# Forgetting attention by head pairs on halves of TensorE, a packed low-rank projection, and another order of the last corrections, in a one-core layer kernel

## The chip, the cores and the metric

The kernel runs on one core of a Trainium2 chip. A core has five engines that run side by side: TensorE (PE; its weight loads are listed apart, as PEld), VectorE (DVE), ScalarE (ACT), GpSimd (POOL) and SyncE (SP). Each works through its own queue in order and waits for the others by semaphores. The metric is the device time of one execution in microseconds (us). Line numbers (L152) are those of the kernel before, unless the text says that they are of the changed kernel.

## What is computed

One layer of a streaming encoder for 512 frames of width 1024, in float32. After a norm, one wide projection feeds three branches (gated linear attention "GLA", forgetting attention "Fox", attention into 256 memory tokens); their outputs are gated and merged, projected and added to the input; a squared-ReLU MLP and a last norm follow. The part that the change touches most is the forgetting attention, 8 heads of 64 channels:

```python
def forgetting_attention(q, k, v, log_f):
    F = jnp.cumsum(log_f, axis=1)                  # per head
    ...
        s = jnp.einsum('bhqd,bhkd->bhqk', qi, kh) * scale
        s = s + Fi[..., None] - F[:, :, None, :]
        mask = k_pos[None, :] <= q_pos[:, None]
        p = jax.nn.softmax(jnp.where(mask, s, -jnp.inf), axis=-1)
        return jnp.einsum('bhqk,bhkd->bhqd', p, vh)
    ...
u = rmsnorm(h, g_mix[l]); proj = u @ w_in[l]       # 2*256+2*512+16+3*512+8+512+3*1024 columns
log_a = log_sigmoid(ga @ w_alpha_up[l] + b_alpha[l]) / GLA_TAU
log_f = log_sigmoid(ff + b_forget[l])
...
h = h + jnp.square(jax.nn.relu(u2 @ w_ff1[l])) @ w_ff2[l]
return rmsnorm(h, g_final)
```

## The kernel before

**Number format.** Large products are made of float32r matmuls. Each operand is split into a rounded part "hi" (a copy on ACT) and the rest "lo" (a subtraction on DVE); `split` (L202) and `split_w` (L139) do it. `mm3` (L150 to L153) then sums hi·hi, hi·lo and lo·hi into one PSUM tile: three matmuls for each 128 rows of contraction. Small products are plain float32.

**Stages, in the order of PE.** A front end (norms, keys and values for the memory), the low-rank and forget columns "G" (L388), the projections for Fox, then Fox itself woven with projections for GLA, memory attention woven with the merge of the Fox branch, GLA woven with the merge of the memory branch, the output projection, and the MLP in four quarters, each a Strassen-like scheme of seven products in the order 1, 2, 5, 6, 3, 7, 4 (L881).

**What sets the order.** PE runs in the order in which the code is written. The other engines' queues are ordered by the build's own scheduler. `weave` (L188) runs a list of attention steps and after each of them fills in its share of 128 units of projection work, a unit being three matmuls.

**G.** `run(gT(("G",), ...))` makes 8 times 3 matmuls from one weight chunk (16 low-rank columns, 8 forget columns, the rest zero) into `gaT`; a row of ones is set there (L383) so that the next small product adds the biases. Its first operand, the normed input `uhi`, `ulo`, is still being made at that time, a k at a time, by DVE (L367 and L204), ACT and POOL. Every weight chunk that goes through `split_w` also counts for `next_sum` (L120), which every second time starts a DMA from POOL that sums weights for the MLP in DRAM (tiles `T`).

**Fox.** `decay_logs` and `decay_sums` make F; `decay_rows` (L422) transposes it and writes -F by four small DMAs from ACT's queue to DRAM (`dF`); each head reads its row back to all partitions (`nFb`, L465). `fox_pair` (L438) projects q and k for two heads and lays them out so that one head uses all 128 rows: in Q the hi part lies on one half of the rows and the lo part on the other, and K's hi (then K's lo) lies on both halves. `fox_scores(h)` (L461) makes for each of four query blocks one matmul with K's hi, one bf16 matmul that adds the causal mask on the last 128 columns (L476), and one matmul with K's lo (L477); DVE adds `nFb` and finds the extreme (L479), ACT takes the exponential (L481), DVE divides by the row sum (L484). `fox_turn(h)` (L487) transposes the blocks on PE and splits them to `PTh`, `PTl`. `fox_values(h)` (L501) multiplies by `V`, whose hi and lo parts fill 64 columns each: eight matmuls a head; ACT and DVE add the two halves (L512, L516). In the woven list, head h's scores, head h-1's transposes and head h-2's values follow each other.

**Last quarter of the MLP.** `evac` (L1038) adds the seven products into the residual tiles `hN`, here `h` (two of them, t = 0 and 1, for each half of the rows; C(i, j, t) is a quarter). Some are added by DMAs from POOL that accumulate in place (`send`, L1035). `finish(t, c, n)` (L1015) takes one 512-column half of a row tile, squares it with a row sum on ACT, multiplies it by the gain, and with n = 1 also norms the tile and writes it out. All `finish` calls stand behind product 7 or 4, the last two.

## Time and profile before

| | |
|---|---|
| median of three timed runs | 855.12 us (853.72 to 855.91) |
| the profiled execution | 855.22 us, of it the span of the trace 853.5 us |
| instructions in the trace | 11749 |
| front end, until G's first matmul | 0 to 40.9 us |
| G and the projections for Fox | 40.9 to 95 us |
| Fox, first scores to last values | 95 to 213 us |
| memory attention and Fox's merge | 213 to 330 us |
| GLA and its merges, output projection, MLP | 330 to 838.2 us |
| after the last matmul | 838.2 to 853.5 us |

In the rows of the profile, a matmul's own duration is longer than the time to the next matmul's start, since matmuls are pipelined; what a stream of them costs is read from starts. A plain float32 matmul shows as two records, a float32r matmul as one. "Idle before" with a releaser says what an engine waited for.

### The profile page before, as it was taken

Reading aid. Unit: us, or ns where it says so; the run is one execution under the profiler, and the core shown is the slowest. Engines: PE = TensorE matmul, PEld = TensorE weight load, DVE = VectorE, ACT = ScalarE, POOL = GpSimd, SP = SyncE. Lnnn points to the kernel's source line nnn. Section 1 sums busy time; section 2 is a strip of 40 time slices with the busy share of each in tenths; the row PEclk is TensorE's granted clock in tenths of the full one; section 3 lists DMA queues with packets and bytes.
Section 4 is the critical chain, followed back from the end, with each engine's and each line's share of the span. In section 5 each row is a group of like instructions: output and inputs, shape, how many; then the busy total and the mean of one; then the engine's idle time right before and its main releaser. Section 6 shows DMA issues by size and latency. Waiting matters only on the chain.

```text
span 853.5 us, 11749 instructions
## 1 busy us (share of the span) xinstructions
PE 827.1 (97%) x4505; PEld 702.7 (82%) x4505; DVE 536.0 (63%) x820; ACT 439.8 (52%) x703; POOL 111.2 (13%) x124
## 2 busy tenths in 40 slices
PE   7999999999999999999999999999999999999992
PEld 5878788888888888878888889887997899799872
DVE  5784656746443545665443548475788678778964
ACT  7765656755233343323323436465676467457744
POOL 5200000000000001222121100111001000100243
PEclk9999999999999999999999999999999999999997
DMA  8444846544636556546322504768758956885694
GB/s 315 154 149 153 205 148 185 142 155 125 195 75 204 192 132 176 130 131 244 102 99 75 196 25 145 210 135 214 234 168 156 277 188 172 184 257 178 136 180 129
DMA packets 37513, 142.37 MB, mean 167 GB/s; under 512 B 4592, under 2 KB 5392, under 8 KB 35728
## 3 DMA queue, kind: packets, MB, share of 16 engines
q1 hardware_dynamic: 27216, 93.36, 31.5%
q0 software_dynamic: 8448, 45.09, 25.7%
q10 hardware_dynamic: 1792, 3.16, 1.2%
q8 instruction: 35, 0.57, 0.3%
q14 instruction: 22, 0.18, 0.1%
HBM read 136.34 MB, written 27.28 MB: 192 GB/s over the span
## 4 chain that ended last, share of the span: by engine, by line
PE 70%; issue 12%; DMA 8%; DVE 4%; ACT 3%; POOL 1%; SPq 0%; POOLq 0%; ACTq 0%; DVEq 0%
PE mm L152 20%; PE mm L151 19%; PE mm L153 19%; DMA b<-in_wst_dram 7%; PE a L152 2%; PE a L151 2%; PE a L153 2%; DVE lo L204 1%; ACT hi L203 1%; DMA h<-s 1%; POOL h L1036 1%; PE a L477 1%; DMA memr<-in_memT_dram 1%; PE a L508 1%; PE a L507 1%
## 5 line engine op out<-in xcount | busy, mean ns | idle before, releaser
L143 DVE TENSOR_TENSOR wlo<-raw,whi 128x1024 fp32r<-128x1024 f32 x80 | 101.4, 1271 | 107.6 <-ACT whi L142 106.6
L142 ACT CAST whi<-raw 128x1024 fp32r<-128x1024 f32 x80 | 84.1, 1052 | 136.4 <-PE mm L152 99.1
L151 PE MATMUL mm<-uhi,whi 128*128 128x512 f32 x360 | 142.6, 396 | 0.0
L152 PE MATMUL mm<-ulo,whi 128*128 128x512 f32 x360 | 140.7, 391 | 1.3 <-DVE ulo L204 1.3
L153 PE MATMUL mm<-uhi,wlo 128*128 128x512 f32 x360 | 140.5, 390 | 0.0
L203 ACT CAST hi<-raw 128x1024 fp32r<-128x1024 f32 x58 | 60.5, 1049 | 44.5 <-PE mm L152 31.6
L204 DVE TENSOR_TENSOR lo<-raw,hi 128x1024 fp32r<-128x1024 f32 x58 | 70.6, 1222 | 17.6 <-ACT hi L203 17.6
L152 PEld LDWEIGHTS mm<-ulo,whi 128*128 128x128 f32 x360 | 67.7, 188 | 15.8 <-DVE ulo L204 2.8
L153 PEld LDWEIGHTS mm<-uhi,wlo 128*128 128x128 f32 x360 | 67.6, 188 | 14.6 <-DVE wlo L143 0.4
L151 PEld LDWEIGHTS mm<-uhi,whi 128*128 128x128 f32 x360 | 67.7, 188 | 13.8 <-issue 0.5
L204 DVE TENSOR_TENSOR lo<-b,hi 128x1024 fp32r<-128x1024 f32 x40 | 48.9, 1223 | 37.2 <-ACT hi L203 37.2
L203 ACT CAST hi<-b 128x1024 fp32r<-128x1024 f32 x40 | 41.9, 1049 | 55.5 <-PE mm L153 22.6
L152 PE MATMUL mm<-lo,ch 128*128 128x512 f32 x160 | 63.0, 394 | 2.7 <-DVE lo L204 2.7
L151 PE MATMUL mm<-hi,ch 128*128 128x512 f32 x160 | 62.4, 390 | 0.0
L1036 POOL DMA_DIRECT2D b<-in_wst_dram x32 | 27.7, 866 | 266.4 <-DVE lo L204 210.4
L153 PE MATMUL mm<-hi,cl 128*128 128x512 f32 x160 | 62.3, 389 | 0.0
L153 PE MATMUL mm<-u2h,lo 128*128 128x256 f32 x192 | 54.3, 283 | 0.0
L152 PE MATMUL mm<-u2l,hi 128*128 128x256 f32 x192 | 54.3, 283 | 0.0
L151 PE MATMUL mm<-u2h,hi 128*128 128x256 f32 x192 | 54.3, 283 | 0.0
L151 PE MATMUL mm<-u2sh,hi 128*128 128x256 f32 x144 | 40.8, 283 | 0.0
L152 PE MATMUL mm<-u2sl,hi 128*128 128x256 f32 x144 | 40.8, 283 | 0.0
L153 PE MATMUL mm<-u2sh,lo 128*128 128x256 f32 x144 | 40.8, 283 | 0.0
(340 smaller groups left out, 1913.1 us busy)
## 6 DMA issues: line engine op xcount, KB each, us to landing
raw<-in_wst_dram SPq DMA_DIRECT2D x122, 512.0 KB, 3.7
b<-in_wst_dram POOLq DMA_DIRECT2D x32, 512.0 KB, 5.5
T<-in_wst_dram POOLq DMA_DIRECT2D x12, 1024.0 KB, 8.5
raw<-T SPq DMA_DIRECT2D x24, 512.0 KB, 3.5
b<-in_wst_dram SPq DMA_DIRECT2D x16, 512.0 KB, 4.9
xr<-in_xT_dram SPq DMA_DIRECT2D x4, 512.0 KB, 8.1
nFb<-dF ACTq DMA_DIRECT2D x8, 256.0 KB, 3.9
h<-in_xN_dram SPq DMA_DIRECT2D x4, 512.0 KB, 7.0
```

The costliest lines, as they stand in the source:

```text
L142: cast = nc.scalar.copy(hi, raw)
L143: nc.vector.tensor_tensor(lo, raw, f(hi), op=ALU.subtract)
L151: nc.tensor.matmul(ps, lh, rh, start=start, stop=False)
L152: nc.tensor.matmul(ps, lh, rl, start=False, stop=False)
L153: nc.tensor.matmul(ps, ll, rh, start=False, stop=stop)
L203: nc.scalar.copy(hi, src)
L204: return nc.vector.tensor_tensor(lo, src, f(hi), op=ALU.subtract).ins
L477: nc.tensor.matmul(ps[:, :w], q, K[e][:, 1, :w], start=False, stop=True)
L507: nc.tensor.matmul(po[:, q0:], vv, PTh[:, c0:c0 + w], start=n == 0, stop=False)
L508: nc.tensor.matmul(po[:, q0:], vv, PTl[:, c0:c0 + w], start=False, stop=n == 3)
L1036: nc.gpsimd.dma_start(to, x, accum_op=ALU.add)
```

## The change

**Fox.** Two heads, which are the two row halves of one projection tile, are now done together. `fox_pair` leaves q and k where the projection puts them (head 0 on rows 0 to 63, head 1 on rows 64 to 127), as tiles hi and lo: two operations for each tile. `fox_scores(j, i)` makes for query block i three float32r matmuls for each head, with 64 rows of contraction, in turn for the two heads and into two PSUM tiles. The mask matmul is gone: -F is written to DRAM in eight slots of 128 (seven writes; three blocks twice), read back as 7 x 128 columns for each head (`fox_rows`), and POOL adds the mask to the copies for the diagonal blocks. `fox_turn(e)` copies the transposed blocks out in float32 without a split. `fox_values(j)` makes plain float32 matmuls with 64 output columns, in turn for the two heads, which land on the two halves of the partitions of one PSUM tile. The woven list has 20 steps in place of 24: transposes of head 0, of head 1, scores for blocks 0 and 1, scores for blocks 2 and 3, values of the pair before.

**G.** The chunk's columns are stored twice; columns 64 to 127 are replaced by their lo part, so that 8 times 2 matmuls do the work, and the biases come in by a column of ones as the bias of the copy out of PSUM. It no longer goes through `split_w`, so it isn't counted for `next_sum`.

**Last quarter.** After product 6 DVE adds G to C(0, 1) itself and `finish(t, 0, 0)` follows at once; after product 3 DVE adds it from PSUM and `finish(t, 1, 1)` follows. Four accumulating DMAs of POOL go, two copies on ACT with them, and all gains are multiplied by DVE.

```diff
-        run(gT(("G",), uhi, ulo, ga_evac))
+        def low_rank():
+            raw = load_w(("G",))
+            both = wp.tile([P, 1024], F32R, tag="hi", name=nm("whi"))
+            raw3, w3 = (t.rearrange("p (k c) -> p k c", k=KT) for t in (raw, both))
+            nc.scalar.copy(both, raw)
+            low = slice(64, P)
+            nc.vector.tensor_tensor(w3[:, :, low], raw3[:, :, low], f(w3[:, :, low]), op=ALU.subtract)
+            ps = mmt()
+            for k in range(KT):
+                nc.tensor.matmul(ps, w3[:, k, :], uhi[:, k, :], start=k == 0, stop=False)
+                nc.tensor.matmul(ps, w3[:, k, :], ulo[:, k, :], start=False, stop=k == KT - 1)
+            nc.scalar.activation(gaT, ps, AF.Identity, bias=ones_row)
...
-            for t in range(NT):
-                nc.scalar.dma_start(dF[:, t * P:(t + 1) * P], nF[8 * t:8 * t + 8, :])
+            for t, (i, j) in enumerate(SLOTS):
+                src = nF[8 * t:8 * t + 8, :]
+                for b in (i, j):
+                    if b is not None:
+                        nc.scalar.dma_start(dF[:, b, :], src)
...
+        def fox_rows(j):
+            live["F", j] = []
+            for e in range(2):
+                h = 2 * j + e
+                F = xp.tile([P, 8, P], F32, tag="nFb", name=nm("nFb"), bufs=4)
+                nc.scalar.dma_start(F[:, :7, :], dF[h:h + 1, :7, :].to_broadcast([P, 7, P]))
+                diag = F[:, 2:8, :].rearrange("p (a b) c -> p a b c", a=2)[:, :, 0:2, :]
+                m = cmask.rearrange("p (a b c) -> p a b c", a=1, b=1).to_broadcast([P, 2, 2, P])
+                nc.gpsimd.tensor_tensor(diag, diag, m, op=ALU.add)
...
-                nc.tensor.matmul(ps[:, :w], q, K[e][:, 0, :w], start=True, stop=False)
-                nc.tensor.matmul(ps[:, n - P:n], cmask, ident16, start=False, stop=False)
-                nc.tensor.matmul(ps[:, :w], q, K[e][:, 1, :w], start=False, stop=True)
+            for a, (q, k) in enumerate(((qh, kh), (qh, kl), (ql, kh))):
+                for e in range(2):
+                    nc.tensor.matmul(pss[e][:, :w], q[half[e], sl], k[half[e], :w], start=a == 0, stop=a == 2)
...
-                nc.tensor.matmul(po[:, q0:], vv, PTh[:, c0:c0 + w], start=n == 0, stop=False)
-                nc.tensor.matmul(po[:, q0:], vv, PTl[:, c0:c0 + w], start=False, stop=n == 3)
+            for kt, c0 in enumerate((0, 512, 1024, 896)):
+                for e in range(2):
+                    nc.tensor.matmul(po[half[e], kt * P:], V[:, kt, 2 * j + e, :], PT[e][:, c0:c0 + S - kt * P],
+                                     start=kt == 0, stop=kt == 3, skip_group_check=True)
+            split(ofh[j], ofl[j], po)
...
-            early = n == 0 or t < 2
+            early = n == 0
...
-                (nc.gpsimd if t < 2 else nc.vector).tensor_tensor(h[c], h[c], g_[c], op=ALU.mult)
+                nc.vector.tensor_tensor(h[c], h[c], g_[c], op=ALU.mult)
...
-                for to, x in ((C(1, 0, t), E), (C(1, 1, t), G), (C(0, 1, t), G)):
+                for to, x in ((C(1, 1, t), G), (C(1, 0, t), E)):
                     send(to, x)
+                add(C(0, 1, t), G)
+                finish(t, 0, 0)
             if n == 3:
+                add(C(0, 1, t), ps)
                 if last:
-                    x = scratch()
-                    nc.scalar.copy(x, ps)
-                    send(C(0, 1, t), x)
-                else:
-                    add(C(0, 1, t), ps)
+                    finish(t, 1, 1)
             if n == 7 and last:
                 add(C(1, 1, t), ps, ALU.subtract)
                 finish(2 + t, 1, 0)
                 add(C(1, 0, t), ps)
-                finish(t, 0, 0)
-                finish(t, 1, 1)
```

On PE, the scores of Fox begin before with these rows for head 0 (`Q` and `K` are its stacked tiles, `cb_s` is the mask and the identity, a_917 and a_926 are the PSUM tiles of query blocks 0 and 1):

```order
L475 MATMUL a_917<-K_566,Q_565 128x256
L476 LDWEIGHTS cb_s
L476 MATMUL a_917<-cb_s 128x128
L477 MATMUL a_917<-K_566,Q_565 128x256
L475 MATMUL a_926<-K_566,Q_565 128x256
```

In the changed kernel, at the same place, stand these for heads 0 and 1 (K_559 and Q_557 are the hi tiles, K_560 and Q_558 the lo tiles; a_899 is head 0's PSUM tile for block 0, a_900 head 1's):

```order
L481 MATMUL a_899<-K_559,Q_557 128x256
L481 MATMUL a_900<-K_559,Q_557 128x256
L481 MATMUL a_899<-K_560,Q_557 128x256
L481 MATMUL a_900<-K_560,Q_557 128x256
L481 MATMUL a_899<-K_559,Q_558 128x256
L481 MATMUL a_900<-K_559,Q_558 128x256
```

For each head and block two long matmuls and a mask matmul have become three long ones, in turn with the other head's. Blocks 0 and 1 of a pair follow each other, blocks 2 and 3 come a step of filling work later.

On DVE, the last rows of the kernel before are these (`lo` are the last weight splits, h_3609 and h_3610 the row tiles 2 and 3, `mm` the products 7 and then 4, `hss` and `ms` the norm's small steps, `gl` the gain):

```order
L204 TENSOR_TENSOR lo_7431<-b_4056,hi_7430 128x1024
L899 TENSOR_TENSOR h_3609<-h_3609,mm_7344 128x512 x2
L899 TENSOR_TENSOR h_3610<-h_3610,mm_7345 128x512 x2
L793 TENSOR_SCALAR hss_3611<-hss_3611 128x1
L1022 TENSOR_TENSOR h_3609<-h_3609,gl 128x512
L793 TENSOR_SCALAR hss_3611<-hss_3611 128x1
L899 TENSOR_TENSOR h_3609<-h_3609,mm_7422 128x512
L793 TENSOR_SCALAR hss_3611<-hss_3611 128x1
L798 TENSOR_SCALAR ms_7387<-hss_3611 128x1
L1022 TENSOR_TENSOR h_3610<-h_3610,gl 128x512
```

In the changed kernel they are (h_3454 to h_3457 are row tiles 0 to 3; mm_7215 and mm_7216 are product 7, mm_7263 and mm_7264 product 4):

```order
L203 TENSOR_TENSOR lo_7272<-b_3903,hi_7271 128x1024
L1043 SCALAR_TENSOR_TENSOR h_3454<-h_3454,rr_7191,gl 128x512
L913 TENSOR_TENSOR h_3456<-h_3456,mm_7215 128x512 x2
L1043 SCALAR_TENSOR_TENSOR h_3455<-h_3455,rr_7208,gl 128x512
L913 TENSOR_TENSOR h_3457<-h_3457,mm_7216 128x512 x2
L807 TENSOR_SCALAR hss_3458<-hss_3458 128x1
L1036 TENSOR_TENSOR h_3456<-h_3456,gl 128x512
L913 TENSOR_TENSOR h_3456<-h_3456,mm_7263 128x512
L807 TENSOR_SCALAR hss_3458<-hss_3458 128x1
L1036 TENSOR_TENSOR h_3457<-h_3457,gl 128x512
L913 TENSOR_TENSOR h_3457<-h_3457,mm_7264 128x512
```

Row tiles 0 and 1 are normed and multiplied ahead of the adds of product 7 and no small step of theirs stands between the adds of product 4 any more. Between the places shown, the queues of DVE, ACT and POOL hold the same operations in the same order in both kernels, apart from the DMAs for `T`, which stand one weight chunk later.

167 lines of the change are left out of this document (78 added, 89 removed).

## The prediction

> **What bounds the kernel now.** I read the busy slices first, then busy time by stretch (start:end, length, then busy time of PE, PEld, DVE, ACT and POOL with counts), then the waits in Fox (95 to 240 us), then the two ends of the change in the timeline.
>
> ```profile
> PE   7999999999999999999999999999999999999992
> ...
> 95.00:213.00 118.00, 117.69 (x609) 97.22 (x608) 75.28 (x194) 73.50 (x148) 5.34 (x8) 1.00 0.53 155
> ...
> 838.20:853.50 15.30, 0.00 (x1) 0.00 (x0) 5.43 (x12) 7.79 (x20) 7.50 (x8) 0.59 0.36 138
> ...
> PE a L491 <- DVE Pt L484: 0.2, 1, 0.2
> ```
>
> In Fox PE has work for 117.7 of 118.0 us and waited 0.2 us for DVE; DVE and ACT are under two thirds. There a microsecond less on PE is a microsecond less of the whole, and what the change takes from DVE and ACT is worth nothing by itself. After the last matmul come 15.3 us in which PE is idle: there the chain through DVE, ACT and POOL counts. The clock in Fox was 1.00.
>
> **Scores of Fox.** One head before, between two projection matmuls (start, duration):
>
> ```profile
> 105.37 0.39 PE L153 MATMUL mm<-uhi,wlo 128*128 128x512 f32 x1
> 105.60 0.28 PE L475 MATMUL a<-K,Q 128*128 128x256 f32 x1
> 105.72 0.23 PE L476 MATMUL a<-cb_s 128*128 128x128 bf16 x1
> ...
> 107.40 0.39 PE L151 MATMUL mm<-uhi,whi 128*128 128x512 f32 x1
> ```
>
> From 105.60 to 107.40 is 1.80 us, eight heads 14.4. The price of a float32r matmul by its width is read from the next start: 0.23 us for 512 columns (105.37 to 105.60), 0.12 for 256 (105.60 to 105.72), and 0.17 for 384 in one head's values:
>
> ```profile
> 111.48 0.39 PE L507 MATMUL a<-PTh,V 128*128 128x512 f32 x1
> ...
> 112.11 0.34 PE L508 MATMUL a<-PTl,V 128*128 128x384 f32 x1
> 112.28 0.28 PE L507 MATMUL a<-PTh,V 128*128 128x256 f32 x1
> ...
> 112.76 0.40 PE L151 MATMUL mm<-uhi,whi 128*128 128x512 f32 x1
> ```
>
> The new scores issue per head three products of widths 256, 256, 384 and 512: 3 x 0.64 = 1.92 us. If two heads on two row halves run at the same time, this is the price of a pair. The trace has no float32r matmul on half the rows; the nearest rows are GLA's float32 ones, on row halves (L735) and on four quarters (L717):
>
> ```profile
> 332.82 0.39 PE L153 MATMUL mm<-uhi,wlo 128*128 128x512 f32 x1
> ...
> 333.14 1.16 PE L735 MATMUL a<-qpos,kn 64*128 64x128 f32 x16
> ...
> 334.57 0.39 PE L152 MATMUL mm<-ulo,whi 128*128 128x512 f32 x1
> ...
> 337.86 1.10 PE L717 MATMUL a<-gv,kdT 64*64 64x128 f32 x32
> ...
> 349.91 1.95 PE L745 MATMUL a<-gv,at 128*128 128x128 f32 x16
> 351.78 1.09 PE L749 MATMUL a<-prev,qpos 64*64 64x128 f32 x28
> ```
>
> From first start to last end, sixteen records on the full array take 1.95 us, sixteen on halves 1.16, thirty-two on quarters 1.10: halves and quarters do overlap. Switching costs something: without the block at 333.14 the matmul at 334.57 would have started two steps of 0.23 after 332.82, at 333.28. The block cost 1.29 us, of which eight records of a half at 0.12 (349.91 to 351.78, a sixteenth) explain 0.9, so 0.4 us go with the entry and the exit of each block. A pair has two blocks (query blocks 0 and 1, then 2 and 3): 1.92 + 0.8 = 2.72 us, four pairs 10.9. **Scores: -3.5 us.** Bounds: no switching cost 7.7 (-6.7), no overlap 4 x (3.84 + 0.8) = 18.6 (+4.2). I take the value by L735, the nearest row.
>
> **Values of Fox.** Before 111.48 to 112.76, 1.28 us, eight heads 10.2. The new ones are float32, two records each, on column halves. A record's price by its width:
>
> ```profile
> L399 PE MATMUL a<-wup_s,gaT x8: 383/386/386, 59.8 to 61.3; 128*128 128x264 f32 x8
> ...
> L717 PEld LDWEIGHTS a<-gv,kdT x64: 129/133/133, 337.9 to 377.2; 64*64 64x64 f32 x64
> ```
>
> Eight records of 264 columns start within 1.5 us, 0.21 us each or 0.81 ns a column; L745 gives 0.9. With 0.84, a head's 512 + 384 + 256 + 128 columns cost 2 x 1280 x 0.84 = 2.15 us, a pair with overlap and 0.4 for switching 2.55, four pairs 10.2. **Values: 0.** Bounds: -1.6 without switching, +8.6 without overlap (4 x 4.7 = 18.8). Column halves alone have no row; L717 needs both kinds of halves to reach 1.10.
>
> A rule of the Trainium skill speaks against this part: "TensorE: Matmul & The Clock Gate", section "Part 3: Packing small matmuls — row/col tiling", says that weight loads overlap running matmuls only where the row group differs. Column halves share all rows. The trace disagrees, since loads for the full array start inside matmuls of the full array:
>
> ```profile
> 334.57 0.19 PEld L153 LDWEIGHTS mm<-uhi,wlo 128*128 128x128 f32 x1
> ```
>
> By the rule the sum would be 8.5 us longer (the rival on loads, below).
>
> **Transposes** stay ten a head. PSUM copies, splits, V's split and the row shuffles of Q and K shrink on DVE and ACT; they were covered and are worth 0. A pair's softmax is now one chain for two heads, but two fill steps and the values of the pair before (two times 128/20 units of 3 x 0.23 us, 8.8, plus 2.5) lie between its last scores and its first transpose. POOL's mask adds (eight, 1.4 us each by POOL's row of L1022 below) lie on an idle engine: 0.
>
> **G.** Eight of 24 matmuls go, 1.8 us. But G waits for its operand:
>
> ```profile
> 37.99 1.21 DVE L143 TENSOR_TENSOR wlo<-raw,whi 128x1024 fp32r<-128x1024 f32 x1
> ...
> 46.54 1.46 DVE L204 TENSOR_TENSOR ulo<-ut,uhi 128x512 fp32r<-128x512 f32 x2
> ...
> 47.28 0.50 PE L152 MATMUL mm<-ulo,whi 128*128 128x512 f32 x1 [0.20 <-DVE ulo L204]
> ...
> 48.09 0.47 PE L152 MATMUL mm<-ulo,whi 128*128 128x512 f32 x1
> ```
>
> The last `ulo` is ready at 48.00, PE uses it at 48.09 and leaves G half a microsecond later. A shorter G only waits longer. What moves that point is G's own split on DVE (37.99), now on half the columns: 1.21 to about 0.7. **G: -0.5 us**; bounds 0 and -1.8.
>
> **The end.** Rows of the tail before:
>
> ```profile
> 837.81 0.39 PE L153 MATMUL mm<-hi,cl 128*128 128x512 f32 x1
> ...
> 837.70 0.63 ACT L791 ACTIVATE sq<-h 128x512 f32<-128x512 f32 x1 [1.55 <-DMA h<-sq]
> ...
> 838.51 4.17 POOL L1022 TENSOR_TENSOR h<-h,gl 128x512 f32<-128x512 f32 x3 [3.32 <-ACT sq L791]
> ...
> 832.30 2.47 DVE L899 TENSOR_TENSOR h<-h,mm 128x512 f32<-128x512 f32 x4
> ...
> 839.87 1.67 DVE L1022 TENSOR_TENSOR h<-h,gl 128x512 f32<-128x512 f32 x1
> ...
> 841.85 0.68 DVE L899 TENSOR_TENSOR h<-h,mm 128x512 f32<-128x512 f32 x1
> ...
> 846.48 0.55 POOL L799 TENSOR_TENSOR rr<-ms,cst_s 128x1 f32<-128x1 f32 x1 [1.02 <-ACT h L1027]
> ...
> 847.06 0.75 DVE L1029 SCALAR_TENSOR_TENSOR h<-h,rr,gl 128x512 f32<-128x512 f32 x1 [0.82 <-POOL rr L799]
> ...
> 828.93 1.23 DVE L204 TENSOR_TENSOR lo<-b,hi 128x1024 fp32r<-128x1024 f32 x1 [1.98 <-ACT hi L203]
> ```
>
> PE ends at 838.2, but the last add on DVE starts at 841.85, behind squares that waited for accumulating DMAs, a gain of 1.67 us beside POOL's, and small steps of the norm. From the end of the last gain (847.81) to the span's end are 5.6 us of output. In the new order, tiles 0 and 1 are done under products 3 and 7, where DVE has gaps (1.98 us ahead of 828.93). DVE's queue from the last split on, by durations above: two gains with norm 0.75 each, four adds 2.47, then small steps (0.3 together), a gain, the add of product 4, a gain and the last add at 0.65 each. From 833.4 (an estimate: the last split, a microsecond later than before, for the new adds stand ahead of it) this is 840.3. Then a square on ACT 0.8, a small step 0.2, POOL 0.56, two gains 1.5 with part of one under POOL: 842.8, and 5.6 of output: 848.4 for 853.5. **The end: -5.0 us**; bounds -3.5 (another 1.5 us of waiting in that queue) and -6.6 (the chain starts at PE's end: 838.2 + 0.7 + 0.8 + 0.2 + 0.6 + 0.75 + 5.6 = 846.9). The added steps delay the splits for products 7 and 4 by up to 2 us; by the same count each is still done 0.6 us or more ahead of PE.
>
> **Sum.** -3.5 + 0 - 0.5 - 5.0 = -9.0 us. The profiled execution took 855.22 us, 0.1 above the median of 855.12: **846.2 us**, a span of 844.5.
>
> **Rivals.** *Row halves of float32r take turns*: scores 18.6 us, +7.7 on the forecast, 853.9. Against it is L735; for it, that no row has this format. *Column halves don't hide their weight loads, or take turns*: 16 loads a pair at 0.133 us, 8.5 us in all, 854.7 (turns: 854.8). Against it are the load at 334.57 and L717. The rule named above would give this. *PE waits in Fox* for a pair's softmax, the masked rows or a PSUM bank: 2 to 5 us, 848 to 851. *Switching is nearly free*: 842.5. *The writes of -F stop ACT*, and the time is longer than before:
>
> ```profile
> 74.65 5.28 ACTq L427 DMA_DIRECT2D dF<-nF  x4
> ...
> 81.59 0.84 ACTq L465 DMA_DIRECT2D nFb<-dF  x2
> ...
> 80.98 0.58 ACT L203 CAST V<-mm 128x512 fp32r<-128x512 f32 x1
> ...
> L427 ACTq DMA_DIRECT2D dF<-nF x4: 318/706/3453, 74.6 to 79.6; - x4
> ...
> 84.12 0.39 PE L151 MATMUL mm<-uhi,whi 128*128 128x512 f32 x1
> ```
>
> Four writes held ACT's queue for 5.28 us, one of them 3.45. Now there are seven, and behind them on ACT stand a cast, the reads of `nFb`, which wait for the writes, and then the copy of V that frees the PSUM bank that PE needs at 84.12. The copy then ends some 3.1 us after the writes (reads issued from 81.59, 1.7 us after the writes' end at 79.93, 0.84 for them, 0.58 for the copy); with PE half a microsecond earlier, writes that end by 80.5 make nothing late. At the mean of 1.3 us a write, seven end at 83.8 and PE waits 3 us: in the case above. At 3.45 each they end at 98.8 and PE waits some 18 us: 864. It is slower from 2.5 us a write on. Against it: three of four were far shorter, and the sum DMA that ran beside them moves away by one weight chunk, since G isn't counted any more.
>
> **How the numbers follow.** Forecast 62%, with 844 to 848.5 as its own range; waits in Fox 12%; cheap switching 6%; row halves 8%; column halves 7%; the writes 5%. From the first three, which hold 80%, the range is 842 to 851.5. Within 0.3% of before (2.6 us, about what this measurement can tell) lie the two tile rivals: same 15%; slower 5%; faster 80%.
>
> **What would show it.** Right: the two heads' score matmuls start within some 10 ns of each other, a pair's scores from first start to the next projection take 1.0 and 1.5 us, values 2.5, G's end moves by half a microsecond, and 10 us remain after the last matmul. Wrong: starts of the halves a full matmul apart; PE idle with DVE, ACT or POOL as its releaser between 84 and 215 us; new waits for `lo` in products 7 and 4; DVE's last add still over 2 us behind the last matmul.

## The result and the profile after

The changed kernel takes **841.87 us** in the median of four runs (841.58 to 842.37), the kernel before beside it 855.51 us (853.72 to 858.64): a ratio of 0.984 (95% interval 0.981 to 0.987). It is faster, by 13.6 us where 9.0 were predicted, and its time lies 0.1 us below the range's low end of 842.0.

The profiled executions (855.22 and 841.72 us) are compared at marks, each the start of a matmul (the last is the end of the span). The row "memory attention to output projection" ends at the first matmul of the MLP. Minus is earlier or shorter.

| mark or stretch | before, us | after, us | difference | forecast |
|---|---|---|---|---|
| front end, to G's first matmul | 40.88 | 39.33 | -1.55 | 0 |
| G, to the decay logs' first matmul | 18.88 | 18.41 | -0.47 | -0.5 |
| decay logs and projections, to the first scores | 35.25 | 35.12 | -0.13 | 0 |
| Fox, to memory attention's first matmul | 136.73 | 132.29 | -4.44 | -3.5 |
| memory attention to output projection | 283.12 | 283.12 | 0 | 0 |
| MLP, to the last matmul | 322.96 | 322.34 | -0.62 | 0 |
| last matmul's start to the span's end | 15.64 | 9.35 | -6.29 | -5.0 |

**Fox.** First PE's busy slices and two stretches of the changed kernel by windows (start:end, length, then busy time of PE, PEld, DVE, ACT and POOL with counts, the granted clock, the DMA share and GB/s), the counterparts of the two rows shown of before:

```profile
PE   7999999999999999999999999999999999999995
...
92.90:206.90 114.00, 114.00 (x611) 88.31 (x611) 60.67 (x167) 54.39 (x117) 13.16 (x14) 1.00 0.57 163
831.00:840.00 9.00, 0.00 (x0) 0.00 (x0) 2.47 (x6) 2.33 (x6) 1.54 (x2) 0.69 0.30 117
```

PE has work in Fox all the time, DVE and ACT about half of it. The scores of the first pair and the values of the first pair in the timeline of the changed kernel (start, duration; L150 to L152 are the three matmuls of a projection step):

```profile
92.55 0.39 PE L152 MATMUL mm<-uhi,wlo 128*128 128x512 f32 x1
92.86 0.97 PE L481 MATMUL a<-K,Q 64*128 64x256 f32 x12
93.76 0.50 PE L150 MATMUL mm<-uhi,whi 128*128 128x512 f32 x1
94.11 0.40 PE L151 MATMUL mm<-ulo,whi 128*128 128x512 f32 x1
...
97.79 0.39 PE L152 MATMUL mm<-uhi,wlo 128*128 128x512 f32 x1
98.11 1.49 PE L481 MATMUL a<-K,Q 64*128 64x384 f32 x12
99.53 0.50 PE L150 MATMUL mm<-uhi,whi 128*128 128x512 f32 x1
99.86 0.40 PE L151 MATMUL mm<-ulo,whi 128*128 128x512 f32 x1
...
126.23 0.39 PE L152 MATMUL mm<-uhi,wlo 128*128 128x512 f32 x1
126.55 2.37 PE L519 MATMUL a<-PT,V 128*64 128x512 f32 x16
128.85 0.50 PE L150 MATMUL mm<-uhi,whi 128*128 128x512 f32 x1
129.19 0.40 PE L151 MATMUL mm<-ulo,whi 128*128 128x512 f32 x1
```

What a block costs is read from the projection matmul before it to the second one after it, less two steps of 0.2275 us: 94.105 - 92.55 - 0.455 = 1.10 us for query blocks 0 and 1, 1.62 for blocks 2 and 3, 2.50 for the values. A pair's scores cost 2.72 us, as forecast to the hundredth; four pairs 10.9 against 14.4. The single records show the overlap (start, duration in ns; the rows don't name the head, it is put in by the order of the code):

```
92.863 381  L481 head 0        126.550 643  L519 head 0
92.866 381  L481 head 1        126.556 643  L519 head 1
93.086 277  L481 head 0        127.030 592  L519 head 0
93.090 277  L481 head 1        127.036 592  L519 head 1
```

The values came out at 2.50 a pair for a forecast of 2.55. Before, a head's values cost 1.29 us by the same measure, so the gain is 0.3 us in all. They also decide on the rule cited in the prediction (the Trainium skill, "TensorE: Matmul & The Clock Gate", Part 3), by which weight loads overlap running matmuls only where the row group differs: by it the time would have been 854.7 us. The loads for the column halves are hidden, as the rows of before said. The same section also lets a load into a background weight buffer go ahead; no row here shows which buffer a load fills, but that sentence would allow what the rows show.

Scores and values make -3.8 us. The rest of Fox's -4.4 lies at a place that the prediction had priced at nothing. The first transposes, before (PE, then ACT):

```profile
99.97 0.39 PE L153 MATMUL mm<-uhi,wlo 128*128 128x512 f32 x1
100.20 0.49 PE L491 MATMUL a<-cst_s,Pt 128*128 128x128 f32 x2
100.93 0.72 PE L491 MATMUL a<-cst_s,Pt 128*128 128x128 f32 x2 [0.24 <-DVE Pt L484]
...
102.06 0.48 PE L151 MATMUL mm<-uhi,whi 128*128 128x512 f32 x1
...
96.77 1.28 ACT L481 ACT_TABLE_LOAD   x1
98.07 0.40 ACT L481 ACTIVATE Pt<-Pt,mx 128x128 f32<-128x128 f32 x1
```

From 100.20 to 102.06 are 1.86 us. In the changed kernel the same ten transposes take 1.01 us (103.75 to 104.76), and so did every later block of before. Before, the softmax of head 0 began with a table load of 1.28 us on ACT and was not done when PE came to transpose it. The view of waits counted 0.2 us for this, because the records of the matmuls, whose ends are modelled, cover most of it; the starts show 0.85. (Scores, values and this make -4.7; some 0.2 us go the other way, spread over the projection matmuls, which start every 0.2282 us on average for 0.2276 before.)

**The end**, in the timeline of the changed kernel (DVE's last weight split and last add, then the chain to the output):

```profile
830.61 0.39 PE L152 MATMUL mm<-hi,cl 128*128 128x512 f32 x1
...
824.17 1.23 DVE L203 TENSOR_TENSOR lo<-b,hi 128x1024 fp32r<-128x1024 f32 x1 [0.36 <-ACT hi L202]
825.32 0.75 DVE L1043 SCALAR_TENSOR_TENSOR h<-h,rr,gl 128x512 f32<-128x512 f32 x1
...
831.04 0.69 DVE L913 TENSOR_TENSOR h<-h,mm 128x512 f32<-128x512 f32 x1
...
831.82 0.63 ACT L805 ACTIVATE sq<-h 128x512 f32<-128x512 f32 x1 [0.63 <-DVE h L913]
...
832.87 0.99 POOL L813 TENSOR_TENSOR rr<-ms,cst_s 128x1 f32<-128x1 f32 x1 [0.39 <-DVE ms L812]
...
833.89 0.75 DVE L1043 SCALAR_TENSOR_TENSOR h<-h,rr,gl 128x512 f32<-128x512 f32 x1 [0.44 <-POOL rr L813]
```

The last add starts 0.43 us behind the last matmul's start (4.04 before). DVE's queue no longer holds it; the chain starts at PE's end.

**The front end**, three stretches by windows (columns as above; the granted clock is the third number from the end), of before and then of after:

```profile
12.00:15.00 3.00, 1.24 (x7) 1.03 (x8) 3.00 (x5) 3.00 (x8) 2.40 (x3) 0.98 1.02 412
15.00:18.00 3.00, 3.00 (x16) 3.00 (x15) 1.36 (x1) 2.21 (x5) 2.92 (x3) 0.50 1.03 411
18.00:21.00 3.00, 3.00 (x26) 3.00 (x26) 0.64 (x2) 1.83 (x4) 1.44 (x3) 0.95 1.03 396
```

```profile
12.00:15.00 3.00, 2.69 (x13) 2.40 (x13) 2.79 (x4) 2.87 (x6) 2.60 (x3) 0.50 1.02 404
15.00:18.00 3.00, 3.00 (x26) 3.00 (x26) 0.85 (x2) 3.00 (x7) 2.92 (x3) 0.97 1.03 416
18.00:21.00 3.00, 3.00 (x27) 3.00 (x27) 2.00 (x2) 2.90 (x7) 2.44 (x3) 1.00 1.03 400
```

Both executions have some 3.4 us in which PE got half its clock. Before, that fell on 15 to 18.3 us, where PE had every operand and did only 16 matmuls in 3 us, for 26 a little later; after, on 11.8 to 15.2, where PE had waits for operands anyway. Just ahead of it the timeline of before has this (DVE, then PE):

```profile
11.48 0.80 DVE L352 CAST cb_s<-cst_s 128x128 bf16<-128x128 f32 x1 [0.31 <-DMA cst_s<-in_cst_dram]
...
13.06 0.38 PE L153 MATMUL mm<-mxh,lo 128*128 128x256 f32 x1 [1.27 <-DVE lo L284]
```

A small copy that waited for the constants' DMA held DVE for 1.0 us, and PE stood 1.27 us behind DVE. It makes the identity in bf16 for the mask matmul (a second one, of 0.22 us at 25.1 us, makes the mask). The change takes both away, and the prediction had no term for it.

### The profile page after: what moved, and what is told of

Same layout as the page of the kernel before. It is cut to its first block, busy times and chain, and to the rows that moved or that the text cites. A ratio compares the mean times of both kernels' runs of the same rounds, so it can differ in the third digit from the quotient of the medians.

```text
span 840.0 us, 11609 instructions
## 1 busy us (share of the span) xinstructions
PE 821.4 (98%) x4497; PEld 691.9 (82%) x4497; DVE 516.8 (62%) x789; ACT 412.2 (49%) x659; POOL 115.2 (14%) x122
## 4 chain that ended last, share of the span: by engine, by line
PE 72%; issue 12%; DMA 7%; DVE 4%; ACT 3%; POOL 1%; POOLq 0%; SPq 0%; ACTq 0%; DVEq 0%
PE mm L150 20%; PE mm L151 20%; PE mm L152 20%; DMA b<-in_wst_dram 7%; PE a L151 2%; PE a L150 2%; PE a L152 2%; DVE lo L203 1%; ACT hi L202 1%; PE a L481 1%; PE a L519 1%; DMA memr<-in_memT_dram 1%; DVE h L913 1%; PE a L749 1%; DVE ulo L203 0%
## 5 line engine op out<-in xcount | busy, mean ns | idle before, releaser
L150 PE MATMUL mm<-uhi,whi 128*128 128x512 f32 x352 | 140.5, 399 | 0.0
L152 PE MATMUL mm<-uhi,wlo 128*128 128x512 f32 x352 | 137.4, 390 | 0.2 <-DVE wlo L142 0.2
L151 PE MATMUL mm<-ulo,whi 128*128 128x512 f32 x352 | 137.3, 390 | 0.0
L150 PEld LDWEIGHTS mm<-uhi,whi 128*128 128x128 f32 x352 | 66.2, 188 | 15.7 <-issue 2.1
L152 PEld LDWEIGHTS mm<-uhi,wlo 128*128 128x128 f32 x352 | 66.1, 188 | 14.8 <-DVE wlo L142 0.6
L150 PE MATMUL mm<-hi,ch 128*128 128x512 f32 x160 | 62.4, 390 | 0.0
L152 PE MATMUL mm<-hi,cl 128*128 128x512 f32 x160 | 62.3, 389 | 0.0
L152 PE MATMUL mm<-u2h,lo 128*128 128x256 f32 x192 | 54.3, 283 | 0.0
L150 PE MATMUL mm<-u2h,hi 128*128 128x256 f32 x192 | 54.3, 283 | 0.0
L150 PE MATMUL mm<-u2sh,hi 128*128 128x256 f32 x144 | 40.8, 283 | 0.0
L152 PE MATMUL mm<-u2sh,lo 128*128 128x256 f32 x144 | 40.8, 283 | 0.0
```

What stands on the lines that cost most here:

```text
L150: nc.tensor.matmul(ps, lh, rh, start=start, stop=False)
L151: nc.tensor.matmul(ps, lh, rl, start=False, stop=False)
L152: nc.tensor.matmul(ps, ll, rh, start=False, stop=stop)
```

## The experiments

"First scores" and the like are the marks of the table. Each run with a time was timed beside the kernel before; its profile was read at the same marks.

### The end

Three kernels take back one part each of the last quarter, a fourth all of it.

```diff
 # tail_undone: evac and finish of the last quarter as in the kernel before
 # adds_only: in evac, after product 6, after product 3, and then after product 7
-                finish(t, 0, 0)
...
-                if last:
-                    finish(t, 1, 1)
...
                 add(C(1, 0, t), ps)
+                finish(t, 0, 0)
+                finish(t, 1, 1)
 # sends_kept: after product 6 and after product 3
-                for to, x in ((C(1, 1, t), G), (C(1, 0, t), E)):
+                for to, x in ((C(1, 0, t), E), (C(1, 1, t), G), (C(0, 1, t), G)):
                     send(to, x)
-                add(C(0, 1, t), G)
                 finish(t, 0, 0)
...
                 if last:
+                    x = scratch()
+                    nc.scalar.copy(x, ps)
+                    send(C(0, 1, t), x)
                     finish(t, 1, 1)
 # pool_gains: in finish
-            early = n == 0
+            early = n == 0 or t < 2
             if early:
-                nc.vector.tensor_tensor(h[c], h[c], g_[c], op=ALU.mult)
+                (nc.gpsimd if t < 2 else nc.vector).tensor_tensor(h[c], h[c], g_[c], op=ALU.mult)
```

> The changed kernel with only the last quarter put back (accumulating DMAs, copies on ACT, gains on POOL, all finish calls at the end). Theory: the new order of the last corrections shortened only the stretch behind the last matmul. That stretch (last matmul's start to the span's end) goes back from 9.4 us to 15.6 +- 0.3, the last matmul itself starts at 830.6 +- 0.4 as in the changed kernel, and the time is 841.9 + 6.3 = 848.2 us. Rival: part of the tail's shortening came from elsewhere (the shift of everything before it against the DMAs): a tail of 12 to 14 us, 845 to 847.

> The changed kernel with the two additions on DVE and all gains on DVE, but tiles 0 and 1 finished behind product 7, as before. Theory A (the DMAs held the squares): below 10.5 us behind the last matmul's start. Theory B (place of the steps): 13 us or more. Six squares of 0.6 us then follow product 7's adds on ACT, and the last add stands behind four gains and a small step that waits for the seventh square: about 11.5 us by these rows.

> The changed kernel with the two additions to C(0,1) done by accumulating DMAs of POOL and copies on ACT, as before, but tiles 0 and 1 still finished behind products 6 and 3, and all gains on DVE. Theory A: what shortened the end is that the accumulating DMAs no longer hold the squares. Then the stretch behind the last matmul's start is back at 13 us or more (of 15.6). Theory B: it is the place of tiles 0 and 1's steps. Then it stays below 10.5 (9.4 in the changed kernel). In DVE's queue two gains with norm, which wait for these DMAs, stand ahead of the last add; by the kernel before the last of these squares came at 837.7, 0.1 us ahead of the last matmul, so I expect 11 to 12, in between.

> The changed kernel with the four gains of row tiles 0 and 1 on POOL again (1.2 to 1.4 us each there, for 0.65 on DVE), additions and finish calls as changed. If the gains on POOL made up a part of the old tail, the stretch behind the last matmul's start grows from 9.35 us by up to 1; if, as the kernel with only the additions (10.1) and the one with the accumulating DMAs kept (13.5) say, the DMAs were what held the end, it stays at 9.3 to 9.5, since these gains now lie beside products 6 to 4.

| kernel | time, us | last matmul's start to the end, us |
|---|---|---|
| changed | 841.87 | 9.35 |
| tail_undone | 847.82 (847.55 to 849.11) | 15.28 |
| adds_only | 844.01 (one run) | 10.10 |
| sends_kept | 851.8 (one run) | 13.46 |
| pool_gains | 843.49 (one run) | 11.00 |

With everything undone the 6 us come back, and the last matmul starts 0.1 us from where it did (830.49 for 830.61): the part's gain is where it was looked for. Keeping only the accumulating DMAs gives 4.1 us back, the gains on POOL alone 1.65, the old place of the steps alone 0.75. My own count had put adds_only and sends_kept both between 11 and 12; the first is lower, the second higher. So theory A holds for the larger part. For pool_gains both expectations missed: I had allowed a growth of at most 1 us. The last three rows are one run each; their stretches are read here, not their times. In sends_kept the DMAs do harm twice (timeline of ACT and PE):

```profile
832.66 0.63 ACT L805 ACTIVATE sq<-h 128x512 f32<-128x512 f32 x1 [4.59 <-DMA h<-sq]
833.20 0.19 ACT L805 ACTIVATION_READ_ACCUMULATOR sq<-h 128x1 f32 x1
833.29 0.56 ACT L1082 COPY sq<-mm 128x512 f32<-128x512 f32 x1
...
833.91 0.50 PE L150 MATMUL mm<-hi,ch 128*128 128x512 f32 x1 [1.49 <-ACT sq L1082]
```

The square waits 4.59 us for a DMA, behind it stands the copy of another product out of PSUM, and behind that PE, which needs the bank.

### The front end

```diff
 # casts_back, casts_back2: the changed kernel with the two operations back
         mk_proj(3)
+        nc.vector.tensor_copy(cb_s[:, 0, :], ident)
+        nc.vector.tensor_scalar(cb_s[:, 1, :], tri, -1.0, -NEG, op0=ALU.add, op1=ALU.mult)
 # before_late_casts: the kernel before with these two behind the last normed input
```

> The changed kernel with the two small DVE operations of the front end put back (identity and mask to bf16, the first of them in DVE's queue ahead of the last operand of the memory projections and waiting for the constants' DMA). Theory: this wait in DVE's queue is what made the front end 1.5 us longer, by moving PE's stall so that the half clock falls on a dense row of matmuls. G's first matmul then starts at 40.9 +- 0.3 us instead of 39.3, and the time is 843.4 us. Rival: the front end's length depends on when the DMAs land in that execution, not on these operations: G's first matmul between 39 and 41 us with no regard to them, and the time 841.9 +- 0.6.

> The kernel before with only these two DVE operations moved behind the last normed input (they are needed only by Fox). Theory of the wait in DVE's queue: G's first matmul at 39.3 +- 0.3 us in place of 40.9, the time 1.5 us below that of the kernel before beside it (ratio 0.998). Rival, landing times of the DMAs: no systematic difference, ratio 1.000, and G's first matmul anywhere between 39 and 41 us.

> The changed kernel once more, to see what varies between its executions, beside the next one on the same chip. If the half clock of 3.4 us in the front end falls anywhere from one execution to the next, G's first matmul is at 38.8 to 39.0 us where it is missing and up to 40.9 where it falls on dense matmuls; Fox, memory attention and GLA keep their lengths (132.3 and 283.1 us) within 0.05 us; the waits for weights in the MLP sum to 0.3 to 2 us; the time is 841.5 to 842.5 us in most executions.

> The changed kernel with the two DVE operations of the front end put back, once more, beside the changed kernel. In its first executions four of six took 843.3 to 843.7 us. Theory: DVE's operation makes PE's stall longer, and with the longer stall the half clock comes in nearly every execution and at a dearer place: a median 1.5 to 2.0 us above that of the changed kernel of the same call, and G's first matmul at 40.4 to 40.9. Rival: the half clock comes by chance in either kernel: medians within 0.6 us, and G's first matmul at 39 or at 40.5 without a rule.

before_late_casts took 853.91 us in the median of twelve runs, the kernel before 855.95 in seventeen: a ratio of 0.9973 (0.9952 to 0.9995), that is 2.0 us, or 0.4 to 4.1 by the interval; G's first matmul came at 38.76, earlier than the 39.3 expected. casts_back took 843.71 (843.29 to 849.81), casts_back2 843.54 (841.88 to 844.54), after_again 842.97 (841.43 to 845.90). So side by side the operations cost only 0.6 us, less than the 1.5 to 2.0 of the theory and as much as its rival allowed. But the last one, the changed kernel itself, scattered more than any theory had said: its profile, of the run of 845.90, had a front end without half clock (39.14), but 39.0 us from the decay logs to the first scores in place of 35.1. That was another matter, and had to be cleared away first.

### What made the changed kernel scatter

The stretch in after_again, timeline of ACT, POOL and PE (ACTq are the DMAs that ACT issues; `T` is a sum DMA for the MLP, issued by POOL):

```profile
78.89 4.54 ACTq L465 DMA_DIRECT2D nFb<-dF  x2
83.47 0.58 ACT L524 COPY V<-mm 128x512 f32<-128x512 f32 x1 [5.73 <-issue]
...
78.05 0.50 POOL L128 DMA_DIRECT2D T<-in_wst_dram  x1 [10.74 <-ACT whi L141]
...
84.11 0.50 PE L150 MATMUL mm<-uhi,whi 128*128 128x512 f32 x1 [2.02 <-ACT V L524]
```

One of the two reads of -F took 4.16 us to issue; the copy of `V` stood behind it and PE behind the copy, and the granted clock behind that was 0.64 from 84 to 87 us. Such a read is in seven of the ten profiles in which G isn't counted for the sum DMAs (in that of after too, where it fell between two copies and held nothing); six of them have PE waiting, and 1.6 to 6 us more in this stretch. In all seven it begins 1.15 to 1.65 us behind the issue of `T` and ends 4.7 to 5.5 us behind it. Not every read at that distance is long: in pool_gains one that came 1.33 us behind `T` took 0.81. Before, one of the *writes* of -F did so (the 3.45 us in the prediction), also beside a `T`. If the neighbour is the cause, moving `T` back moves the long issue.

```diff
 # g_counted: the changed kernel, with G's chunk counted for the sum DMAs again
-            nc.scalar.copy(both, raw)
+            next_sum(nc.scalar.copy(both, raw).ins)
```

> The changed kernel with G's weight chunk counted again for the sum DMAs of POOL, as before, so that these start where they did. Theory: in the changed kernel one of the first four reads of -F takes 3.5 to 4.2 us to issue on ACT whenever it comes more than 1.2 us behind a sum DMA (issued at 78.0 us), and the copy of V behind it then holds PE, by 1.6 to 3.9 us in four of seven profiles. Counted again, the sum DMA is issued at about 72.3 us, beside the writes of -F as in the kernel before; one write takes 3 to 4 us, no read does, and the stretch from the decay logs' first matmul to the first scores is 35.1 us. No execution is above 843.5 us, the median 841 to 842. Rival: the long issue comes from the reads themselves (448 KB each, four in a row) or from the weights' DMAs: it stays at the reads, and the stretch is 37 to 39 us in some executions.

> The kernel with G counted, once more, beside the filled one on the same chip: median 841.2 to 841.9, no read of -F above 1 us, the stretch from the decay logs' first matmul to the first scores 35.1 us, G's first matmul at 38.6 to 39.4 us.

g_counted took 841.57 us (841.06 to 841.93) and again 841.98 (841.48 to 842.25), ten runs within 1.2 us; the stretch is 35.14 us in both profiles. The timeline of the first:

```profile
71.65 6.28 ACTq L439 DMA_DIRECT2D dF<-ab  x7
77.97 1.05 ACT L141 CAST whi<-raw 128x1024 fp32r<-128x1024 f32 x1 [6.35 <-DMA dF<-ab]
...
80.06 0.84 ACTq L465 DMA_DIRECT2D nFb<-dF  x2
...
71.77 0.50 POOL L128 DMA_DIRECT2D T<-in_wst_dram  x1 [12.60 <-ACT ab L434]
```

`T` is at 71.77, one of the seven writes takes 3.33 us, and no read is long. A cast on ACT stands behind the writes, but PE doesn't wait for it. In all six profiles with G counted (these two and four below) one write takes 3.3 to 3.6 us, beginning 1.45 us behind `T`, and no read of the first four more than 0.9. The theory holds. The median is no lower than the changed kernel's best runs, but none of the ten runs is above 842.25, while four of the changed kernel's nine are, up to 845.90. Why a write some 8 us behind `T` took 1.2 to 2.8 us in seven of the ten profiles without the counting stays open; PE didn't wait for it.

### The front end again

On this steadier kernel the two operations were put back, and PE's waits in the front end were filled with matmuls of zeros.

```diff
 # counted_casts: g_counted and the two operations
 # counted_casts_filled, counted_filled: with and without the operations, and in mm3
+        for _ in range(FILL.get(step_n[0], 0)):     # {0: 1, 2: 1, 4: 2, 6: 4, 8: 3}
+            nc.tensor.matmul(at_(), wz[:, :P], wz, start=True, stop=True)
+        step_n[0] += 1
```

> The kernel with G counted (841.1 to 841.9 us in five executions, no long read of -F any more) with the two DVE operations of the front end put back. Theory: the wait of DVE's first one for the constants makes PE's stalls at 11 to 15 us longer, and in most executions the half clock of 3.4 us then falls on the dense matmuls behind them: G's first matmul at 40.4 to 41 us in most, a median of 843 to 843.5. Rival: the half clock comes as often without them, and the operations cost nothing: median 841.2 to 842.0. In profiles without half clock G's first matmul comes at 38.7 to 39.1 us with or without them, so by either theory that is where it is when the profile shows none.

> The same with eleven idle matmuls (zeros, not read; bf16 128x512, 0.22 us each) put on PE where it waits for the memory projections' operands. Theory: the half clock follows a stretch in which PE does little. With the waits filled, the clock stays at 1.00 from 6 to 34 us, G's first matmul is at 38.7 to 39.3 us and the median 841.2 to 842.0, as without the two DVE operations. Rival: the half clock doesn't depend on these waits: still about as often, and the median at or above that of the run without filling, since the idle matmuls delay the others by up to 0.2 us at five places.

> The kernel with G counted and the eleven idle matmuls in the front end's waits, without the two DVE operations. If the idle matmuls themselves cost time later on (with the operations the filled kernel took 845.0 us in place of 843.4, though its profile had a front end without half clock), the median is 843 to 845. If the loss there belonged to the operations, it is 841.0 to 842.0, as without filling.

counted_casts took 843.43 us (842.50 to 846.94, six runs). Without the operations, beside it on the same chip, counted_values_behind (below) took 841.56 (841.04 to 842.46); that kernel's Fox is also 0.56 us shorter, for another reason. Against g_counted itself, on other chips, the difference is 1.9 and 1.5 us, and before_late_casts says 2.0 for the kernel before. **The two operations cost some 1.5 to 2 us**; the size is not known better than that. All unfilled profiles, with the half clock of the front end and the start of G:

| operations | profile | half clock from (for), us | G's first matmul, us |
|---|---|---|---|
| at their old place | before | 14.9 (3.4) | 40.88 |
| | casts_back | 14.2 (3.4) | 40.42 |
| | casts_back2 | 9.3 (10.2) | 41.81 |
| | counted_casts | 15.5 (3.4), 29.2 (6.8) | 43.96 |
| | before_step_between | none | 38.94 |
| gone or later | g_counted_again, no_turns | 9.0, 9.2 (6.8 each) | 39.56, 39.61 |
| | adds_only, pool_gains | 9.3, 9.3 (3.4 each) | 38.75, 38.86 |
| | counted_values_behind, after | 11.4, 11.8 (3.4 each) | 39.15, 39.33 |
| | values_behind_scores | 27.8 (3.4) | 40.58 |
| | five others | none | 38.69 to 39.14 |

Up to some 14 us PE has waits for operands anyway, and a half clock that falls there costs little; one that falls behind them, on dense matmuls, costs 1.5 us and more. With the operations it came later or lasted longer in four of five profiles. Without half clock G comes at 38.9 with the operations as well, though in one profile only: by this the wait itself costs nothing, and the half clock costs what is lost. That is the reading that fits the table; why the wait should shift the half clock isn't shown.

That PE's idleness brings the half clock isn't shown either. With the waits filled the clock was 1.00 through the front end in both profiles (G at 39.10 and 38.49), as expected; but the times were 845.03 us (842.72 to 847.36) with the operations and 843.76 (841.14 to 847.05) without, worse than unfilled. The profile of the first loses 3.5 us in the MLP, to one wait of 1.3 us for a weight's hi part and a half clock behind it; that of the second, 841.14 us, loses nothing. What the slower ones lost was not seen and stays open.

### Fox

```diff
 # before_step_between: the kernel before, an empty step behind head 0's scores
+                    if len(steps) == 1:
+                        steps.append(lambda: None)
 # no_turns: three matmuls of head 0, then three of head 1
-            for a, (q, k) in enumerate(((qh, kh), (qh, kl), (ql, kh))):
-                for e in range(2):
+            for e in range(2):
+                for a, (q, k) in enumerate(((qh, kh), (qh, kl), (ql, kh))):
 # values_behind_scores; counted_values_behind with G counted as well
+                if a[1] == 2 and a[0] > 0:
+                    fox_values(a[0] - 1)
...
+        steps = [s for s in steps if s.args[0] is not fox_values or s.args[1] == 3]
```

> The kernel before with an empty step in the woven list behind head 0's scores, so that twice the filling work lies between them and head 0's transposes. Theory: in the kernel before the first transposes waited 0.85 us for the softmax of head 0 (its block costs 1.95 us where the other seven cost 1.10), which the two steps of scores in the changed kernel cover. The first block of transposes costs 1.10 us, and first scores to the memory attention's first matmul is 0.8 to 0.9 us shorter (135.9 for 136.7). Rival: the first block is slow for another reason, such as a first use of the buffers or of the exponential's table: it stays at 1.9 us and the stretch keeps its length.

> The changed kernel with the scores' matmuls not in turn: three for head 0, then three for head 1, on the same row halves and into the same two PSUM tiles. Theory: two matmuls overlap only when they follow each other directly on different halves of the rows. Then only one pair in six overlaps: blocks 0 and 1 of a pair of heads cost 1.1 + 0.5 = 1.6 us or a little more (for 1.11), blocks 2 and 3 cost 1.62 + 0.8 = 2.4 or more, and Fox is at least 4 x 1.3 = 5 us longer (137.5 for 132.3). Rival: PE looks further ahead and overlaps them whatever the order: Fox stays at 132.3.

> The changed kernel with the values of the pair before put straight behind a pair's scores for blocks 2 and 3, with no filling matmuls between (three of the four values blocks; 17 steps in place of 20). Theory: each block on halves costs 0.4 us more than its streams, half of it on the way in and half on the way out, so that three joined blocks save 0.4 us each: Fox 131.1 us for 132.3. Rival: going from row halves in float32r to column halves in float32 costs as much as going through the full array: 132.3. A third: the values' PSUM tile must wait for DVE's reading of the first scores just made: 132.3 to 134.

> The kernel with G counted and three of the four values blocks straight behind the scores. Each joined block saved 0.18 us and Fox was 131.69 for 132.29 us, so the median should be 0.6 us below that of the kernel with G counted: 840.9 to 841.2. Rival: what Fox saves is given back in waits for the weights in the MLP (3.3 to 3.8 us there in the profiles without disturbance): 841.5.

*The first transposes.* With the empty step their block costs 1.10 us in place of 1.95, so the 0.85 us were a wait for head 0's softmax and not the place's own. The stretch got only 0.25 us shorter, because that one execution (856.28 us) has another wait in Fox, 0.51 us ahead of a projection matmul at 159.96.

*Turns.* Without turns the scores cost 1.12 and 1.62 us a block, as with them, and Fox stays at 132.34: the theory that the order makes the overlap fell. The second head's first matmul, three places behind in PE's queue, starts 10 ns after the first head's (3 ns with turns). The block of the first pair in the timeline, for the one at 92.86 above:

```profile
98.77 0.39 PE L152 MATMUL mm<-uhi,wlo 128*128 128x512 f32 x1
99.08 0.98 PE L481 MATMUL a<-K,Q 64*128 64x256 f32 x12
99.99 0.50 PE L150 MATMUL mm<-uhi,whi 128*128 128x512 f32 x1
100.33 0.40 PE L151 MATMUL mm<-ulo,whi 128*128 128x512 f32 x1
```

The run took 848.04 us, 6 of them in the stretch with a long read of -F.

*Joined blocks.* Scores for blocks 2 and 3 with the values straight behind cost 3.94 us where apart they cost 1.62 + 2.50 = 4.12. I had expected 0.4 less and got 0.18; by this the way from row halves to column halves costs 0.2 by itself. Fox took 131.69 us (131.75 with G counted) for 132.29. The one run of values_behind_scores, 847.38 us, has a long read of -F and says nothing of the time. In time the gain cannot be told from g_counted: 841.56, where 840.9 to 841.2 were expected, against 841.57 and 841.98, not side by side. No version here is clearly faster than the changed kernel's better runs.

## Why the prediction was off

The profiled executions are 13.5 us apart, 4.5 more than forecast. Of these the front end is 1.55, the end 1.3, Fox 0.9 and the MLP 0.6, all of one sign. The range's low end came from a single rival, free switching, and left no room for a term that had no price, nor for several small ones together.

**What held.** The scores: -3.48 us for -3.5, with the overlap read from float32 blocks of another stage and 0.4 us for each way on and off the halves. G: -0.47 for -0.5 (the other profiles of the changed kernel and its variants have 18.35 to 18.81 us there, so up to 0.4 of it is chance); PE now waits longer for its operand, as said. The values: -0.3 for 0, inside 0.05 us a pair. (From the first start to the next projection matmul, as the signs were worded, the blocks take 0.90, 1.42 and 2.30 us for 1.0, 1.5 and 2.5, since a part of the way off the halves shows only at the matmul after that.) No engine made PE wait in Fox, and the splits for products 7 and 4 were in time.

**The step that failed: the front end was taken as unchanged.** The prediction priced what replaces the mask matmul (the rows of -F, POOL's adds), but not what made its operands, two small operations on DVE, of which the first, at 11.5 us, waits for a DMA. This wait was in the profile of before, ahead of a stall of PE of 1.27 us, and the granted clock of 0.50 from 15 to 18 us stood in the windows; neither went into the sum, which put the front end at 0 without a reason. It is worth 1.55 us between the two profiles and some 1.5 to 2 in medians. With that the forecast would have been 844.2 to 844.7, still over 2 us above the measured time.

**A wait read too small.** "They were covered and are worth 0" was right of the transposes but one: the first block of before waited 0.85 us, of which the view of waits shows 0.2.

**The end was mis-sized**: -6.3 (-5.9 when undone) for -5.0. Of the 1.3 us, 0.8 is the last split, for which I had assumed a microsecond of delay: it ends 5.2 us ahead of the last matmul's start, for 5.4 before. Another 0.6 is DVE's queue, 6.3 us from there to the end of the last add where I had counted 6.9, since adds follow each other every 0.6 us; the chain behind the last add is 0.1 longer than forecast. The bound of -6.6 was the better reading: the chain starts at PE's end.

**The MLP's -0.6** stays open. PE's waits there are mostly for the lo parts of weights on DVE. The changed kernel and g_counted, two profiles each, have 322.3 to 322.6 us there; the kernel before and its two variants 323.0, 323.7 and 325.4; but other variants of the changed kernel reach 323.2, or 324.5 in sends_kept with the wait shown above, and 326.3 with the filling. Nothing was tried to find out whether the changed kernel is steadily better there.

**The rivals.** Row halves taking turns, and column halves with bare weight loads: refuted. Free switching: refuted; the blocks cost what the 0.4 us said. The writes of -F stopping ACT: the mechanism is real, but I had it at the wrong DMA. I counted the move of the sum DMA as evidence against it; the move took the long issue from the writes, behind which nothing was urgent, to the reads, with the copy of `V` and PE behind them. Where it strikes it costs 1.6 to 6 us, not 18, and the nine runs' medians of 841.87 and 842.97 hide most of it.

## What to carry to other kernels

Search the whole program for what the change takes away, the makers of a removed operand above all: here a copy of 0.8 us, which waited for a DMA ahead of something that PE needed, went with 1.5 to 2 us. Read what a wait costs from the starts of the neighbours, not from the view of waits, where the records' modelled ends cover most of it. When a change shifts a counter that paces background DMAs, ask what these now run beside; and where the profiled runs of one kernel differ by 4 us, find that cause before measuring anything smaller.

## What the runs showed of the hardware

- *The half clock.* In the front end it came in 11 of the 19 profiles, for some 3.4 us at a time (6.8 or 10.2 in four), at a place that moved from execution to execution. It came later too: behind a wait of 2 us (after_again, at 84.8 us), and in G, in ten profiles, behind two waits of 0.9 and 0.65 us. The Trainium skill ("TensorE: Matmul & The Clock Gate", Part 1) describes a free-running window of 3.4 us and a fall to half rate after an idle one; the length and the wandering agree, but in before PE had been busy for 1.24 of the 3 us ahead of it and never idle for more than 1.27 at a time. In values_behind_scores PE was even busy for 3.0 of the 3.4 us ahead of it (27.8 us, by the records' durations).
- *DMA issue.* In 16 of the 19 profiles one issue on ACT took 3.3 to 4.2 us, instead of mostly 0.3 to 0.5; it came 1.15 to 1.65 us behind a 1 MB DRAM-to-DRAM DMA from POOL and ended 4.7 to 5.5 us behind it. It moved with that DMA. Two issues at that distance were not long (0.81 us in pool_gains, 0.36 in casts_back, where the next one was). ACT's instructions behind it waited too.
- *Overlap on row halves.* Float32r matmuls on the two row halves start 3 to 4 ns apart and cost together what one costs (0.117 us a pair for 256 columns, for 0.12 on the full array). PE starts a matmul on free row halves ahead of two that stand before it in the code (no_turns, 10 ns behind the first head's, by the order of the rows).
- *Ways between tilings.* From the full array to row halves and back 0.4 us together (1.10 us for a block whose streams are 6 x 0.117); from row halves to column halves about 0.2 (3.94 joined, 4.12 apart).
